# Turning the operands of an SSD stage in 32x32 blocks on VectorE and over DRAM, in place of TensorE transposes

## The chip, the core and the metric

The kernel runs on one core of a Trainium2 chip: TensorE (PE, with its weight loads shown as PEld), VectorE (DVE), ScalarE (ACT), GpSimd (POOL) and SyncE (SP), which here only starts transfers. The metric is the device time of one execution in microseconds (us).

## The reference

One layer of a generator: 256 latent and 256 context tokens of width 2048 (512 tokens in all) are normed and modulated, projected by `w_in`, passed through a two-way Mamba-2 scan (the SSD part: 32 heads in 8 groups, state 128, chunks of 128 tokens) and a gated MLP, and projected back. What matters here is the SSD part:

```python
z = h @ w_in                                   # 512 tokens, channels of x, B, C first
xbc = silu(dwconv(z[..., :XBC_W]))             # 5 taps along the tokens
# x: 2048 channels (256 a group), B and C: 128 channels a group
states = einsum('bckgn,bckgr,bckgrp->bcgrpn', B, decay_to_end, x * dt)   # sums over tokens k
h_starts = scan(states)                        # context first, then the latent chunks
y_diag = einsum('bcqgn,bckgn,bcgrqk,bckgrp->bcqgrp', C, B, L, x * dt)    # sums over tokens k
y_off  = einsum('bcqgn,bcgrpn,bcqgr->bcqgrp', C, h_starts, exp(acs))
y = y_diag + y_off + d_skip * x                # forward and backward in time, latent tokens only
```

The projection leaves channels on the partitions and tokens along the row. The sums over tokens want x and B with tokens on the partitions, so each is transposed; and the diagonal part comes out with channels on the partitions and is transposed back.

## The kernel before

**Projection.** Weights are kept as fp32 and split into a high and a low part (`hi_w` by ACT at L542, `lo_w` by DVE at L548, halves of 128x1024). A product of 128 channels by 512 tokens over 2048 inputs is 16 steps of three TensorE products each (`mm3`, L141 to L143): 48 products of 128x512, into one PSUM tile `psx`. The SSD stage lies between about 125 and 455 us. Its outer loop runs over 25 channel tiles (`REST`); seven more were projected earlier. Tile 4g and 4g+1 are x of group g, 4g+2 is B, 4g+3 is C; C tiles are of 256 latent tokens only, so their products are 128x256.

**Small work in between.** All that happens to a tile after its projection is put between the products of later tiles by a plan written by hand: `later(t, fn)` notes that `fn` is to be emitted `t` units from now, and `pump(dt)` after each six products moves the plan's clock by 1.3 units (0.65 for a C tile) and emits what is due. A tile of 48 products is so 10.4 units. The order in which instructions are emitted is kept on PE, DVE, ACT and POOL: each engine runs its list in that order and waits at the first instruction whose input is not there.

**One group.** `conv_tile` does the convolution: the middle tap on ACT (L607), the others on DVE (L623), silu on ACT (L626). Then:

- `ssd_x`: four TensorE transposes of 128x128 per x tile into PSUM (`ptx`, L742), which ACT copies to `xk` (L746); `xk` is x with tokens on the partitions.
- `ssd_w`: POOL scales `xk` to `xw` and `xl` (L754, L757); `ssd_sk`: POOL writes `d_skip * x` into `y` (L870).
- `ssd_b`: the same four transposes for B (`ptb`, L765; copy by ACT to `bk`, L770).
- `ssd_cb`: products of C and B (`pcb`, L808); `ssd_states`: products of `bk` with `xw` and `xl` (`psc` L825, `psl` L828). Then the states `hs`, the masks `M` and `E`, the products `pso` with C, and POOL's adds of those into `y` (`ssd_ya`).
- `ssd_yd`: the diagonal part (`psy`, L904); `ssd_yc`: ACT copies it to SBUF (`yc`); `ssd_yt`: four transposes (`pty`, L918); `ssd_yf`: DVE adds it to `y` (L922).

`plan_tile` (at the end of the listing) places these: B is transposed 7 units after its projection, the states come 6 units after C's (plus `late`, which is 10 for the first groups and 0 for the others).

The weights come by SP's queue (1 MB per tile). POOL's queue holds, in this stage, only `acs` (a table written to DRAM at L709) and `R` (its rows, read back to all partitions at L724, once per group). In a later stage of the same kernel the latent `y` and `vt` are turned in another way: DVE transposes 32x32 blocks within 128x512 (L1062, tile `T`), and 16 POOL transfers of 256 pieces of 128 B (L1067, tile `Z`) put the blocks to their places.

Of the kernel before, what the change touches and what calls it, by code (L numbers as in the profile page):

```python
# [8 lines left out]
F32 = mybir.dt.float32  # L9
# [11 lines left out]
NGRP = 8  # L21
# [26 lines left out]
def tile_hybrid_ssd_mlp(  # L48
# [47 lines left out]
    y = ypool.tile([P, 2, D], F32, tag="big16", name="y")  # L96
# [29 lines left out]
    dsk = cpool.tile([P, 32], F32, name="dsk")  # L126
# [45 lines left out]
    def spt(shape, name):  # L172
        return sps.tile(shape, F32, tag="s", name=name)
# [162 lines left out]
    for k in range(KT):  # L336
# [7 lines left out]
        g = k % 4  # L344
# [249 lines left out]
    def conv_tile(i, src, d0, ds):  # L594
        ch = ORDER[i]
        lat = ch >= 24
        n = 256 if lat else 512
        cw = pc[:, C_CW + 5 * i : C_CW + 5 * i + 5]
        l0 = 0 if lat else 256
        T = {}  # L600

        def tap0():
            if ch < 16:
                o = cv3.tile([P, n], F32, tag="xs", name=f"xbc{i}")
            else:
                o = cv2.tile([P, n], F32, tag="cs" if lat else "bs", name=f"xbc{i}")
            nc.scalar.activation(o, src, AF.Identity, bias=pc[:, C_CB + i : C_CB + i + 1], scale=cw[:, 2:3])  # L607
            T["o"] = o

        def taps():  # L610
            o = T["o"]
            o4 = o[:, l0 : l0 + 256].rearrange("p (r t) -> p r t", r=4)
            src4 = src[:, l0 : l0 + 256].rearrange("p (r t) -> p r t", r=4)
            for k in (0, 1, 3, 4):
                s = k - 2
                parts = [(o4, src4, 64)]
                if not lat:
                    parts.append((o[:, 0:256], src[:, 0:256], 256))
                for (a, z, w) in parts:
                    o0, o1 = max(0, -s), w - max(0, s)  # L620
                    ao = a[..., o0:o1]
                    zi = z[..., o0 + s : o1 + s]
                    nc.vector.scalar_tensor_tensor(ao, zi, cw[:, k : k + 1], ao, op0=ALU.mult, op1=ALU.add)  # L623

        def silu():
            nc.scalar.activation(T["o"], T["o"], AF.Silu)  # L626
            done[i] = T["o"]

        later(d0, tap0)
        later(d0 + 0.9, taps)  # L630
        later(d0 + ds, silu)
# [97 lines left out]
    gs_ = {}  # L729

    def hp(ap):
        return ap.rearrange("p (h q) -> p h q", h=4)

    def ssd_x(g, xi):
        S = gs_.setdefault(g, {})
        if xi == 0:
            S["xk"] = cv2.tile([P, 4, 256], F32, tag="xk", name=f"xk{g}")
        xk = S["xk"]
        xt = done.pop(4 * g + xi)
        p = spt([P, 4, P], f"ptx{g}{xi}")  # L740
        for t in range(4):
            nc.tensor.transpose(p[:, t, :], xt[:, t * P : (t + 1) * P], ident)  # L742
        S["ptx", xi] = p

    def ssd_xc(g, xi):
        nc.scalar.copy(gs_[g]["xk"][:, :, xi * P : (xi + 1) * P], gs_[g]["ptx", xi])  # L746

    def ssd_w(g):
        S = gs_[g]
        xk, h4 = S["xk"], slice(4 * g, 4 * g + 4)  # L750
        xw = cv1.tile([P, 2, 2, 256], F32, tag="xw", name=f"xw{g}")
        for t in range(2):
            for d in range(2):
                nc.gpsimd.tensor_tensor(hp(xw[:, t, d, :]), hp(xk[:, t, :]), bc(wctx(t, d)[:, h4], 2, 64), op=ALU.mult)  # L754
        xl = cv1.tile([P, 2, 256], F32, tag="xl", name=f"xl{g}")
        for d in range(2):
            nc.gpsimd.tensor_tensor(hp(xl[:, d, :]), hp(xk[:, 2 + d, :]), bc(wlt(d)[:, h4], 2, 64), op=ALU.mult)  # L757
        S["xw"], S["xl"] = xw, xl

    def ssd_b(g):  # L760
        bt = done[4 * g + 2]
        bk = cv1.tile([P, 4, P], F32, tag="bk", name=f"bk{g}")
        p = spt([P, 4, P], f"ptb{g}")
        for t in range(4):
            nc.tensor.transpose(p[:, t, :], bt[:, t * P : (t + 1) * P], ident)  # L765
        S = gs_.setdefault(g, {})
        S["bk"], S["ptb"] = bk, p

    def ssd_bc(g):
        nc.scalar.copy(gs_[g]["bk"], gs_[g]["ptb"])  # L770


    def ssd_d(g, c, h2):
# [91 lines left out]
    def yg(g, c):  # L865
        return y[:, c, g * 256 : (g + 1) * 256]

    def ssd_sk(g):
        for c in range(2):
            nc.gpsimd.tensor_tensor(hp(yg(g, c)), hp(gs_[g]["xk"][:, 2 + c, :]), bc(dsk[:, 4 * g : 4 * g + 4], 2, 64),  # L870
                                    op=ALU.mult)

    def ssd_o(g):
        S = gs_[g]
# [14 lines left out]
    def ssd_ya(g, c):  # L889
        yo = gs_[g]["yo", c]  # L890
        for d in range(2):
            nc.gpsimd.tensor_tensor(yg(g, c), yg(g, c), yo[:, d, :], op=ALU.add)
# [3 lines left out]
    def ssd_yd(g):  # L896
        S = gs_[g]
        E, xk = S["E"], S["xk"]
        ps = spt([P, 2, 2, P], f"psy{g}")
        for c in range(2):  # L900
            for q in range(2):
                for hh in range(2):
                    h = 2 * q + hh
                    nc.tensor.matmul(ps[64 * hh : 64 * hh + 64, c, q, :], lhsT=xk[:, 2 + c, h * 64 : (h + 1) * 64],  # L904
                                     rhs=E[:, c, h, :], start=True, stop=True)
        S["psy"] = ps

    def ssd_yc(g):
        S = gs_[g]
        S["yc"] = cv1.tile([P, 2, 2, P], F32, tag="M", name=f"yc{g}")  # L910
        nc.scalar.copy(S["yc"], S["psy"])

    def ssd_yt(g):
        S = gs_[g]
        S["pty"] = spt([P, 2, 2, P], f"pty{g}")
        for c in range(2):
            for q in range(2):
                nc.tensor.transpose(S["pty"][:, c, q, :], S["yc"][:, c, q, :], ident)  # L918

    def ssd_yf(g):  # L920
        ya = y[:, :, g * 256 : (g + 1) * 256]
        nc.vector.tensor_tensor(ya, ya, gs_[g]["pty"].rearrange("p c q k -> p c (q k)"), op=ALU.add)  # L922

    def plan_tile(i, src, d0=0.0, ds=5.2, tx=7.0, tw=1.5, late=0.0, td=0.0):

        g, r = divmod(i, 4)
        conv_tile(i, src, d0, ds)
        if r < 2:
            later(d0 + tx, lambda: ssd_x(g, r))
            later(d0 + tx + 0.7, lambda: ssd_xc(g, r))  # L930
        if r == 1:
            later(d0 + tx + tw, lambda: ssd_w(g))
            later(d0 + tx + tw + 3, lambda: ssd_sk(g))
        if r == 2:
            later(d0 + tx, lambda: ssd_b(g))
            later(d0 + tx + 0.7, lambda: ssd_bc(g))
        if r == 3:
            d0 += late
            for t, fn in [(6, ssd_cb), (6, ssd_states), (6.9, ssd_cbm), (7.6, lambda g: ssd_mb(g, 0)), (8, ssd_hc),
                          (8.7, ssd_hd), (9.4, ssd_hl), (9.5, lambda g: ssd_m(g, 0)), (11.2, lambda g: ssd_mb(g, 1)),  # L940
                          (12, ssd_o), (12.2, lambda g: ssd_m(g, 1)), (13.9, lambda g: ssd_yo(g, 0)),
                          (14.5, lambda g: ssd_yo(g, 1)), (14.7, lambda g: ssd_ya(g, 0)), (15.3, lambda g: ssd_ya(g, 1)),
                          (16 + td, ssd_yd), (16.9 + td, ssd_yc),
                          (18.6 + td, ssd_yt), (19.3 + td, ssd_yf)]:
                later(d0 + t, lambda fn=fn: fn(g))
            plan_d(d0 + 11, g + 1, 1.5)
            plan_e(d0 + 17, g + 1)
# [192 lines left out]
    for blk in range(16):  # L1140
# [85 lines left out]
    for i in range(8):  # L1226
        tk, b = divmod(i, 4)
# [156 lines left out]
```

## Time and profile before

| | before |
|---|---|
| median of 3 runs | 978.47 us (978.17 to 980.12) |
| profiled execution | 981.04 us, span 979.3 us, mean granted TensorE clock 0.996 |
| DVE, ACT, POOL busy | 68%, 51%, 19% of the span |
| a 1 MB weight load, issue to landing | 4.8 us (median of 25) |

In the rows of the trace the first number is the start in us, the second the time (of a group: all its instructions), then engine, line, operation, output<-inputs, shape and count; what stands in brackets is the idle time just ahead of it and what ended it. L12 is line 12 of the kernel that the row belongs to. The span runs from the first to the last instruction; the execution's time has some 1.7 us around it.

### The profile page before, as it was taken

The numbers are of one execution on the slowest core, as the hardware profiler recorded it, in microseconds if no ns is written. First come the engines' busy times: TensorE is split into PE (matmuls) and PEld (weight loads), VectorE is DVE, ScalarE is ACT, GpSimd is POOL, SyncE is SP. The second block draws the span as 40 slices with busy tenths as digits, with TensorE's granted clock in tenths as the row PEclk, the third lists the DMA queues.
The fourth block names the chain that finished last, engine by engine and source line by source line (L and its number), as shares of the span: only waits on it lengthen the run. The fifth ranks groups of instructions, "written<-read, shape, count | busy, mean of one in ns | idle before, by whom it ended". The sixth has DMA issues, their size and how long they took to land.

```text
span 979.3 us, 13757 instructions
## 1 busy us (share of the span) xinstructions
PE 968.3 (99%) x5242; PEld 781.8 (80%) x5242; DVE 665.1 (68%) x1075; ACT 496.0 (51%) x757; POOL 186.6 (19%) x290
## 2 busy tenths in 40 slices
PE   9999999999999999999999999999999999999997
PEld 4688888787887878787888888886888888888885
DVE  6888798778876665755766776666666665445636
ACT  4344458666565454645444443444566564345522
POOL 0000002541462122124000000043333451000000
PEclk9999999999999999999999999999999999999999
DMA  9999953332333423146787778785666666556722
GB/s 366 417 415 415 371 217 130 110 133 86 129 106 132 151 86 130 47 169 221 300 301 281 266 255 309 269 302 168 213 209 199 235 219 207 201 186 241 271 89 86
DMA packets 37090, 211.45 MB, mean 216 GB/s; under 512 B 6417, under 2 KB 6673, under 8 KB 14369
## 3 DMA queue, kind: packets, MB, share of 16 engines
q1 hardware_dynamic: 30240, 192.91, 53.2%
q0 software_dynamic: 6208, 16.85, 5.2%
q8 instruction: 41, 0.67, 0.3%
q10 hardware_dynamic: 576, 0.82, 0.2%
q14 instruction: 25, 0.20, 0.1%
HBM read 204.20 MB, written 2.16 MB: 211 GB/s over the span
## 4 chain that ended last, share of the span: by engine, by line
PE 78%; DMA 11%; DVE 6%; issue 3%; ACT 2%; POOL 0%; SPq 0%; DVEq 0%; ACTq 0%; POOLq 0%
PE psx L141 9%; PE psx L143 9%; PE psx L142 9%; PE pa L1159 7%; PE pa L1160 7%; PE pa L1161 7%; DMA gate<-in_wada_dram 5%; PE pm L1202 3%; PE pm L1201 3%; PE pm L1200 3%; DMA ada<-in_wada_dram 3%; DVE lo_w L88 3%; PE pq L1202 2%; PE pq L1201 2%; PE pq L1200 2%
## 5 line engine op out<-in xcount | busy, mean ns | idle before, releaser
L88 DVE TENSOR_TENSOR lo_w<-w,hi_w 128x1024 fp32r<-128x1024 f32 x173 | 209.7, 1221 | 127.9 <-ACT hi_w L87 127.9
L87 ACT CAST hi_w<-w 128x1024 fp32r<-128x1024 f32 x173 | 181.9, 1053 | 210.5 <-PE pa L1161 146.3
L1159 PE MATMUL pa<-hi_w,hhi 128*128 128x512 f32 x512 | 201.7, 394 | 0.0
L1160 PE MATMUL pa<-lo_w,hhi 128*128 128x512 f32 x512 | 200.2, 391 | 1.3 <-DVE lo_w L88 1.3
L1161 PE MATMUL pa<-hi_w,hlo 128*128 128x512 f32 x512 | 199.9, 390 | 0.0
L141 PE MATMUL psx<-hhi,hi_w 128*128 128x512 f32 (+1 forms) x400 | 153.4, 383 | 0.0
L143 PE MATMUL psx<-hhi,lo_w 128*128 128x512 f32 (+1 forms) x400 | 145.9, 365 | 0.0
L142 PE MATMUL psx<-hlo,hi_w 128*128 128x512 f32 (+1 forms) x400 | 145.7, 364 | 0.0
L1160 PEld LDWEIGHTS pa<-lo_w,hhi 128*128 128x128 f32 x512 | 96.4, 188 | 21.8 <-DVE lo_w L88 2.0
L1159 PEld LDWEIGHTS pa<-hi_w,hhi 128*128 128x128 f32 x512 | 96.5, 189 | 21.4 <-issue 1.6
L1161 PEld LDWEIGHTS pa<-hi_w,hlo 128*128 128x128 f32 x512 | 96.5, 189 | 20.3
L623 DVE SCALAR_TENSOR_TENSOR xbc<-psx,pc,xbc 128x248 f32<-128x248 f32 (+1 forms) x204 | 83.6, 471 | 34.5 <-ACT xbc L607 33.5
L548 DVE TENSOR_TENSOR lo_w<-w,hi_w 128x1024 fp32r<-128x1024 f32 x61 | 77.1, 1271 | 23.7 <-ACT hi_w L542 23.6
L1067 POOL DMA_DIRECT2D Z<-T x128 | 73.9, 584 | 97.4 <-DVE T L1062 28.8
L141 PEld LDWEIGHTS psx<-hhi,hi_w 128*128 128x128 f32 x400 | 75.5, 189 | 13.3 <-issue 2.9
L143 PEld LDWEIGHTS psx<-hhi,lo_w 128*128 128x128 f32 x400 | 75.4, 189 | 12.5
L142 PEld LDWEIGHTS psx<-hlo,hi_w 128*128 128x128 f32 x400 | 75.6, 189 | 12.2 <-issue 1.7
L542 ACT CAST hi_w<-w 128x1024 fp32r<-128x1024 f32 x61 | 63.5, 1044 | 26.0 <-PE psx L142 12.9
L1013 DVE SCALAR_TENSOR_TENSOR junk<-gate,cb 128x2048 bf16<-128x2048 f32 x16 | 36.7, 2291 | 27.9 <-DMA gate<-in_wada_dram 27.9
L1200 PE MATMUL pm<-hi_w,hhi 128*128 128x512 f32 x128 | 49.8, 389 | 0.0
L1201 PE MATMUL pm<-lo_w,hhi 128*128 128x512 f32 x128 | 49.8, 389 | 0.0
L1202 PE MATMUL pm<-hi_w,hlo 128*128 128x512 f32 x128 | 49.8, 389 | 0.0
(270 smaller groups left out, 1398.9 us busy)
## 6 DMA issues: line engine op xcount, KB each, us to landing
w<-in_wlat_dram SPq DMA_DIRECT2D x64, 1024.0 KB, 4.9
w<-in_wout_dram SPq DMA_DIRECT2D x32, 1024.0 KB, 4.8
w<-in_wxbc_dram SPq DMA_DIRECT2D x25, 1024.0 KB, 4.8
ada<-in_wada_dram SPq DMA_DIRECT2D x24, 1024.0 KB, 13.9
gate<-in_wada_dram SPq DMA_DIRECT2D x16, 1024.0 KB, 5.9
ada<-in_wada_dram SPq DMA_DIRECT2D x16, 512.0 KB, 12.3
R<-acs POOLq DMA_DIRECT2D x8, 1024.0 KB, 5.7
wst<-in_wst_dram SPq DMA_DIRECT2D x15, 480.0 KB, 12.9
```

Source lines behind the costliest of these rows:

```text
L87: nc.scalar.copy(hi, raw)
L88: nc.vector.tensor_tensor(lo, raw, hi.bitcast(F32), op=ALU.subtract)
L141: nc.tensor.matmul(ps, lhsT=whi, rhs=hhi[k][:, s], start=start, stop=False)
L142: nc.tensor.matmul(ps, lhsT=whi, rhs=hlo[k][:, s], start=False, stop=False)
L143: nc.tensor.matmul(ps, lhsT=wlo, rhs=hhi[k][:, s], start=False, stop=stop)
L623: nc.vector.scalar_tensor_tensor(ao, zi, cw[:, k : k + 1], ao, op0=ALU.mult, op1=ALU.add)
L1159: nc.tensor.matmul(pa[tk], lhsT=hhi[k][:, t], rhs=whi[:, w], start=k == 0, stop=False)
L1160: nc.tensor.matmul(pa[tk], lhsT=hhi[k][:, t], rhs=wlo[:, w], start=False, stop=False)
L1161: nc.tensor.matmul(pa[tk], lhsT=hlo[k][:, t], rhs=whi[:, w], start=False, stop=k == KT - 1)
L1200: nc.tensor.matmul(p, lhsT=yh[:, t], rhs=whi[:, w], start=j == 0, stop=False)
L1201: nc.tensor.matmul(p, lhsT=yh[:, t], rhs=wlo[:, w], start=False, stop=False)
L1202: nc.tensor.matmul(p, lhsT=yl[:, t], rhs=whi[:, w], start=False, stop=hf == 0 and j == 15)
```

## The change

x of groups 1 to 7, and B and y of groups 1 to 6, are no longer transposed by TensorE: 26 tiles of 128x512, 104 transposes, and the 26 copies by ACT. Instead `turn` has DVE transpose the tile in 32x32 blocks (`STREAM_TRANSPOSE`, into a tile `tt` of which there is one buffer; for y it reads PSUM and writes `yc`) and POOL write it to a scratch `D` in DRAM (two buffers), as 2048 pieces of 128 B. `turned` reads it back by four POOL transfers of 512 pieces of 128 B, one per 32 partitions, into `xk`, `bk` or a tile `yz`. Group 0, and B and y of group 7, stay on TensorE. `xk` gets another layout (x tile, token tile, channel) and its readers follow.

The plan moves with it: the reads are emitted 5 units (`LAND`) after the write, `xw` waits 13 units in place of 1.5 where x goes over DRAM, and `late` is at least 4 where B does, so that the states and all behind them come 4 units later in groups 2, 4, 5 and 6 (groups 1 and 3 had 10 and keep it).

```diff
+    def by_pe(g, what):
+        return g == 0 or g == NGRP - 1 and what != "x"
+
+    def turn(T, src, nm):
+        nc.vector.transpose(T.rearrange("p (b g c) -> p g b c", b=4, g=4), src.rearrange("p (g b c) -> p g b c", g=4, b=4))
+        D = drt.tile([64, 1024], F32, tag="D", name=f"D{nm}")
+        nc.gpsimd.dma_start(D.rearrange("(b g a) (i c) -> (a i) (b g) c", b=4, g=4, c=32),
+                            T.rearrange("p (u c) -> p u c", c=32))
+        return D
+
+    def turned(dst, D):
+        for b in range(4):
+            nc.gpsimd.dma_start(dst[32 * b : 32 * b + 32].rearrange("p (u c) -> p u c", c=32),
+                                D[16 * b : 16 * b + 16, :].rearrange("u (i c) -> i u c", c=32))
...
     def ssd_x(g, xi):
...
         xt = done.pop(4 * g + xi)
+        if not by_pe(g, "x"):
+            T = cv1.tile([P, 512], F32, tag="tt", name=f"tx{g}{xi}")
+            S["Dx", xi] = turn(T, xt, f"x{g}{xi}")
+            return
...
     def ssd_xc(g, xi):
-        nc.scalar.copy(gs_[g]["xk"][:, :, xi * P : (xi + 1) * P], gs_[g]["ptx", xi])
+        xk = gs_[g]["xk"][:, xi]
+        if by_pe(g, "x"):
+            nc.scalar.copy(xk, gs_[g]["ptx", xi])
+        else:
+            turned(xk.rearrange("p t c -> p (t c)"), gs_[g]["Dx", xi])
...
     def ssd_b(g):
+        if not by_pe(g, "b"):
+            T = cv1.tile([P, 512], F32, tag="tt", name=f"tb{g}")
+            S["Db"] = turn(T, bt, f"b{g}")
+            return
...
     def ssd_yc(g):
-        nc.scalar.copy(S["yc"], S["psy"])
+        if by_pe(g, "y"):
+            nc.scalar.copy(S["yc"], S["psy"])
+        else:
+            S["Dy"] = turn(S["yc"].rearrange("p c q k -> p (c q k)"), S["psy"].rearrange("p c q k -> p (c q k)"), f"y{g}")

     def ssd_yt(g):
+        if not by_pe(g, "y"):
+            S["pty"] = cv1.tile([P, 2, 2, P], F32, tag="yo0", name=f"yz{g}")
+            turned(S["pty"].rearrange("p c q k -> p (c q k)"), S["Dy"])
+            return
...
+    LAND = 5.0
+
     def plan_tile(i, src, d0=0.0, ds=5.2, tx=7.0, tw=1.5, late=0.0, td=0.0):
...
+        lx, lb, ly = (0.7 if by_pe(g, w) else LAND for w in "xby")
+        if lx == LAND:
+            tw = max(tw, 2 * LAND + 3)
+        if lb == LAND:
+            late = max(late, 4.0)
         if r < 2:
             later(d0 + tx, lambda: ssd_x(g, r))
-            later(d0 + tx + 0.7, lambda: ssd_xc(g, r))
+            later(d0 + tx + lx, lambda: ssd_xc(g, r))
...
         if r == 2:
             later(d0 + tx, lambda: ssd_b(g))
-            later(d0 + tx + 0.7, lambda: ssd_bc(g))
+            later(d0 + tx + lb, lambda: ssd_bc(g))
...
                           (16 + td, ssd_yd), (16.9 + td, ssd_yc),
-                          (18.6 + td, ssd_yt), (19.3 + td, ssd_yf)]:
+                          (16.9 + td + (1.7 if ly < 1 else LAND), ssd_yt), (18.6 + td + (0.7 if ly < 1 else 2 * LAND), ssd_yf)]:
```

How the lists read at the places that the prediction speaks of. Numbers behind a name tell buffers of one name apart; the first number is the group or, for `psx`, `xbc` and `lo_w`, the channel tile or the weight half.

TensorE before, in the tile after C of group 6 (`psx28`, whose products run over the inputs `hhi0` to `hhi15`):

```order
L143 MATMUL psx28_3764<-hhi9_125,lo_w43_3725 128x512
L808 MATMUL pcb6_3817<-xbc27_3771,xbc26_3699 128x128 x2
L825 MATMUL psc6_3820<-xw6_3678,bk6_3787 128x512 x2
L828 MATMUL psl6_3823<-xl6_3683,bk6_3787 128x256 x2
L141 MATMUL psx28_3764<-hhi10_126,hi_w43_3701 128x512
```

TensorE now:

```order
L143 MATMUL psx28_3800<-hhi15_131,lo_w43_3757 128x512
L848 MATMUL pcb6_3885<-xbc27_3807,xbc26_3732 128x128 x2
L865 MATMUL psc6_3888<-xw6_3840,bk6_3823 128x512 x2
L868 MATMUL psl6_3891<-xl6_3845,bk6_3823 128x256 x2
L141 MATMUL psx29_3894<-hhi0_116,hi_w44_3777 128x512
```

The states of group 6 stood after 30 of that tile's 48 products (`hhi9` is the tenth input), and stand after all 48.

DVE now, from the first split (`lo_w43`) in that tile on; `xbc27` are the taps of C, `tb6` the block transpose of B, `yz5` the diagonal part of group 5 back from DRAM:

```order
L968 TENSOR_TENSOR y_68<-y_68,yz5_3685 128x2x256
L549 TENSOR_TENSOR lo_w43_3757<-w21_3457,hi_w43_3734 128x1024
L549 TENSOR_TENSOR lo_w44_3791<-w22_3565,hi_w44_3777 128x1024
L624 SCALAR_TENSOR_TENSOR xbc27_3807<-psx27_3725,pc_87,xbc27_3807 128x4x62
L624 SCALAR_TENSOR_TENSOR xbc27_3807<-psx27_3725,pc_87,xbc27_3807 128x4x63 x2
L624 SCALAR_TENSOR_TENSOR xbc27_3807<-psx27_3725,pc_87,xbc27_3807 128x4x62
L549 TENSOR_TENSOR lo_w45_3821<-w22_3565,hi_w45_3809 128x1024
L739 STREAM_TRANSPOSE tb6_3824<-xbc26_3732 128x4x4x32
L549 TENSOR_TENSOR lo_w46_3865<-w23_3697,hi_w46_3857 128x1024
```

Before, the splits, the taps and the next split stood there in the same order, without the first row and without the transpose.

POOL before, from the last add of group 5 to the states of group 6 (`M60` is a mask, `hs6` the states):

```order
L892 TENSOR_TENSOR y_68<-y_68,yo51_3537 128x256 x2
L724 DMA R7_3586<-acs_1459 128x2048
L754 TENSOR_TENSOR xw6_3678<-xk6_3579,ed_1458 128x256 x4
L757 TENSOR_TENSOR xl6_3683<-xk6_3579,ed_1458 128x256 x2
L870 TENSOR_TENSOR y_68<-xk6_3579,dsk_108 128x256 x2
L853 TENSOR_TENSOR M60_3838<-cbb6_3835,dtt_1457 128x512
```

POOL now, the same stretch:

```order
L741 DMA Dy5_3643<-yc5_3641 128x16x32
L725 DMA R7_3650<-acs_1461 128x2048
L747 DMA xk6_3590<-Dx60_3593 32x16x32 x4
L747 DMA yz5_3685<-Dy5_3643 32x16x32 x4
L741 DMA Dx61_3711<-tx61_3709 128x16x32
L747 DMA xk6_3590<-Dx61_3711 32x16x32 x4
L741 DMA Db6_3826<-tb6_3824 128x16x32
L786 TENSOR_TENSOR xw6_3840<-xk6_3590,ed_1460 128x256 x4
L789 TENSOR_TENSOR xl6_3845<-xk6_3590,ed_1460 128x256 x2
L747 DMA bk6_3823<-Db6_3826 32x16x32 x4
```

`xw6` and `xl6` now stand behind eleven transfers of POOL, the write of B last among them, and the four reads of `bk6` follow them. In group 2 the write of the next x stands between:

```order
L741 DMA Db2_2420<-tb2_2418 128x16x32
L786 TENSOR_TENSOR xw2_2436<-xk2_2143,ed_1460 128x256 x4
L789 TENSOR_TENSOR xl2_2441<-xk2_2143,ed_1460 128x256 x2
L741 DMA Dx30_2458<-tx30_2456 128x16x32
L747 DMA bk2_2417<-Db2_2420 32x16x32 x4
```

Before, no transfer stood there but those of `R`.

More of the change, by code (lines that the diff above doesn't have):

```diff
@@ L516, in tile_hybrid_ssd_mlp @@
     drp = ctx.enter_context(mkpool(name="drp", bufs=1, space=bass.MemoryType.DRAM))
+    drt = ctx.enter_context(mkpool(name="drt", bufs=2, space=bass.MemoryType.DRAM))
     cv1 = cvs.enter_context(mkpool(name="cv1", bufs=1))
@@ L736, in ssd_x @@
         if xi == 0:
-            S["xk"] = cv2.tile([P, 4, 256], F32, tag="xk", name=f"xk{g}")
-        xk = S["xk"]
+            S["xk"] = cv2.tile([P, 2, 4, P], F32, tag="xk", name=f"xk{g}")
         xt = done.pop(4 * g + xi)
+        if not by_pe(g, "x"):
+            T = cv1.tile([P, 512], F32, tag="tt", name=f"tx{g}{xi}")
+            S["Dx", xi] = turn(T, xt, f"x{g}{xi}")
+            return
         p = spt([P, 4, P], f"ptx{g}{xi}")
@@ L745, in ssd_xc, with xtok_, hx, hb @@
     def ssd_xc(g, xi):
-        nc.scalar.copy(gs_[g]["xk"][:, :, xi * P : (xi + 1) * P], gs_[g]["ptx", xi])
+        xk = gs_[g]["xk"][:, xi]
[3 more added lines that the diff above has]
+            turned(xk.rearrange("p t c -> p (t c)"), gs_[g]["Dx", xi])
+    def xtok_(g, t):
+        return gs_[g]["xk"][:, :, t].rearrange("p x (h q) -> p x h q", h=2)
+    def hx(ap):
+        return ap.rearrange("p (x h q) -> p x h q", x=2, h=2)
+    def hb(ap):
+        return bc(ap.rearrange("p (x h) -> p x h", x=2), 3, 64)
     def ssd_w(g):
         S = gs_[g]
-        xk, h4 = S["xk"], slice(4 * g, 4 * g + 4)
+        h4 = slice(4 * g, 4 * g + 4)
         xw = cv1.tile([P, 2, 2, 256], F32, tag="xw", name=f"xw{g}")
@@ L753, in ssd_w @@
             for d in range(2):
-                nc.gpsimd.tensor_tensor(hp(xw[:, t, d, :]), hp(xk[:, t, :]), bc(wctx(t, d)[:, h4], 2, 64), op=ALU.mult)
+                nc.gpsimd.tensor_tensor(hx(xw[:, t, d, :]), xtok_(g, t), hb(wctx(t, d)[:, h4]), op=ALU.mult)
         xl = cv1.tile([P, 2, 256], F32, tag="xl", name=f"xl{g}")
         for d in range(2):
-            nc.gpsimd.tensor_tensor(hp(xl[:, d, :]), hp(xk[:, 2 + d, :]), bc(wlt(d)[:, h4], 2, 64), op=ALU.mult)
+            nc.gpsimd.tensor_tensor(hx(xl[:, d, :]), xtok_(g, 2 + d), hb(wlt(d)[:, h4]), op=ALU.mult)
         S["xw"], S["xl"] = xw, xl
@@ L761, in ssd_b @@
         bt = done[4 * g + 2]
-        bk = cv1.tile([P, 4, P], F32, tag="bk", name=f"bk{g}")
+        S = gs_.setdefault(g, {})
+        S["bk"] = cv1.tile([P, 4, P], F32, tag="bk", name=f"bk{g}")
+        if not by_pe(g, "b"):
+            T = cv1.tile([P, 512], F32, tag="tt", name=f"tb{g}")
+            S["Db"] = turn(T, bt, f"b{g}")
+            return
         p = spt([P, 4, P], f"ptb{g}")
@@ L765, in ssd_b @@
             nc.tensor.transpose(p[:, t, :], bt[:, t * P : (t + 1) * P], ident)
-        S = gs_.setdefault(g, {})
-        S["bk"], S["ptb"] = bk, p
+        S["ptb"] = p
     def ssd_bc(g):
-        nc.scalar.copy(gs_[g]["bk"], gs_[g]["ptb"])
+        bk = gs_[g]["bk"]
+        if by_pe(g, "b"):
+            nc.scalar.copy(bk, gs_[g]["ptb"])
+        else:
+            turned(bk.rearrange("p t c -> p (t c)"), gs_[g]["Db"])
     def ssd_d(g, c, h2):
@@ L869, in ssd_sk @@
         for c in range(2):
-            nc.gpsimd.tensor_tensor(hp(yg(g, c)), hp(gs_[g]["xk"][:, 2 + c, :]), bc(dsk[:, 4 * g : 4 * g + 4], 2, 64),
-                                    op=ALU.mult)
+            nc.gpsimd.tensor_tensor(hx(yg(g, c)), xtok_(g, 2 + c), hb(dsk[:, 4 * g : 4 * g + 4]), op=ALU.mult)
     def ssd_o(g):
@@ L903, in ssd_yd @@
                     h = 2 * q + hh
-                    nc.tensor.matmul(ps[64 * hh : 64 * hh + 64, c, q, :], lhsT=xk[:, 2 + c, h * 64 : (h + 1) * 64],
+                    nc.tensor.matmul(ps[64 * hh : 64 * hh + 64, c, q, :], lhsT=xk[:, q, 2 + c, hh * 64 : (hh + 1) * 64],
                                      rhs=E[:, c, h, :], start=True, stop=True)
@@ L910, in ssd_yc @@
         S["yc"] = cv1.tile([P, 2, 2, P], F32, tag="M", name=f"yc{g}")
-        nc.scalar.copy(S["yc"], S["psy"])
+        if by_pe(g, "y"):
+            nc.scalar.copy(S["yc"], S["psy"])
+        else:
+            S["Dy"] = turn(S["yc"].rearrange("p c q k -> p (c q k)"), S["psy"].rearrange("p c q k -> p (c q k)"), f"y{g}")
     def ssd_yt(g):
         S = gs_[g]
+        if not by_pe(g, "y"):
+            S["pty"] = cv1.tile([P, 2, 2, P], F32, tag="yo0", name=f"yz{g}")
+            turned(S["pty"].rearrange("p c q k -> p (c q k)"), S["Dy"])
+            return
         S["pty"] = spt([P, 2, 2, P], f"pty{g}")
```

## The prediction

> **What bounds the kernel now.** I read the page first, then the SSD stage (about 125 to 455 us) by stretches, since the edits lie only there.
>
> ```profile
> PE 968.3 (99%) x5242; PEld 781.8 (80%) x5242; DVE 665.1 (68%) x1075; ACT 496.0 (51%) x757; POOL 186.6 (19%) x290
> PEclk9999999999999999999999999999999999999999
> 200.00:240.00 40.00, 40.00 (x214) 32.60 (x213) 30.53 (x62) 24.93 (x45) 12.09 (x17) 1.00 0.28 106
> 400.00:440.00 40.00, 40.00 (x217) 33.28 (x216) 24.23 (x41) 20.84 (x29) 8.89 (x13) 1.00 0.37 132
> ```
>
> The columns of the last two are the stretch, its length, busy time of PE, PEld, DVE, ACT and POOL, the granted clock, the DMA share and GB/s. TensorE is never idle in these 40 us and runs at full clock. DVE has 9 to 16 us of room, POOL 28, ACT 15. So whatever is taken from TensorE's list shortens the kernel one for one, and any moment at which TensorE must wait lengthens it one for one. A transfer costs nothing until TensorE's next instruction needs it.
>
> **What the removed work is worth.** The timeline of PE around one removed turn, and the one wait that goes with it:
>
> ```profile
> 260.33 0.39 PE L142 MATMUL psx<-hlo,hi_w 128*128 128x512 f32 x1
> 260.56 0.40 PE L143 MATMUL psx<-hhi,lo_w 128*128 128x512 f32 x1
> 260.79 0.60 PE L742 MATMUL ptx<-ident,xbc 128*128 128x128 f32 x4
> 261.15 0.47 PE L141 MATMUL psx<-hhi,hi_w 128*128 128x512 f32 x1
> 261.46 0.39 PE L142 MATMUL psx<-hlo,hi_w 128*128 128x512 f32 x1
> PE ptx L742 <- ACT xbc L626: 0.5, 1, 0.5
> ```
>
> Matmuls are pipelined, so I count starts, not durations. Products of 128x512 start 0.23 us apart (260.33 to 260.56). From 260.56 to 261.46 are 0.90 us, in which two products (0.45) and the four transposes stand: 0.45 us for a turn. Of x there are 2 x 7 turns, of B 6, of y 6: 26 x 0.45 = 11.7 us. The wait at `ptx` (x of group 1, 0.5 us) goes too. Gain: 12.2 us. The 26 copies by ACT that go are worth nothing: ACT is not waited for elsewhere on this path.
>
> **What is added, and what hides it.** DVE gets 26 block transposes, POOL 26 writes and 104 reads of DRAM. On average there is room. For x of groups 2 to 7, used a tile or more later, and for y, which only `yf` on DVE awaits, I take 0: POOL's and DVE's idle time covers it. Not so for B: `bk` is an operand of the states `psc`, and TensorE takes its list in order. In the new order `psc` of groups 2, 4, 5 and 6 stands behind all 48 products of the tile after C (before: behind 30). Group 6, on the clock of the old trace:
>
> ```profile
> 380.22 0.40 PE L141 MATMUL psx<-hhi,hi_w 128*128 128x512 f32 x1
> 387.53 0.60 PE L808 MATMUL pcb<-xbc,xbc 128*128 128x128 f32 x4
> 387.97 1.02 PE L825 MATMUL psc<-xw,bk 128*128 128x512 f32 x2
> ```
>
> That tile begins at 380.22. 48 x 0.227 (10.9) bring `pcb` to 391.1, and its 0.44 (387.53 to 387.97) bring `psc` to 391.55. That is when `bk6` is due. What stands ahead of it:
>
> ```profile
> 378.60 2.35 DVE L548 TENSOR_TENSOR lo_w<-w,hi_w 128x1024 fp32r<-128x1024 f32 x2
> 381.03 2.02 DVE L623 SCALAR_TENSOR_TENSOR xbc<-psx,pc,xbc 128x248 f32<-128x248 f32 x4
> 382.96 1.22 DVE L548 TENSOR_TENSOR lo_w<-w,hi_w 128x1024 fp32r<-128x1024 f32 x1
> L922 DVE TENSOR_TENSOR y<-y,pty x8: 674/687/690, 192.3 to 454.2; 128x512 f32<-128x512 f32 x8
> L1062 DVE STREAM_TRANSPOSE T<-vt x8: 666/702/712, 642.3 to 713.9; 128x512 f32<-128x512 f32 x8
> 372.59 2.33 POOL L754 TENSOR_TENSOR xw<-xk,ed 128x256 f32<-128x256 f32 x4 [10.31 <-ACT xk L746]
> 374.89 1.18 POOL L757 TENSOR_TENSOR xl<-xk,ed 128x256 f32<-128x256 f32 x2
> L1067 POOL DMA_DIRECT2D Z<-T x128: 584/584/612, 647.1 to 812.0; - x128
> L709 POOL DMA_DIRECT2D acs<-y x1: 651/651/651, 135.3 to 135.3; - x1
> ```
>
> In DVE's new order `yf` of group 5 (0.69) stands ahead of the two splits, so these run from 379.3 to 381.6, the C taps (2.02) to 383.6, `lo_w45` (1.22) to 384.8, and `tb6`, priced as the transposes of the later stage (0.70), to 385.5. POOL issues `Db6` (0.58) till 386.1, and then must do `xw6` and `xl6` (2.33 + 1.18) before its four reads of `bk6`: 389.6. The reads need `Db6` landed.
>
> Issue times: the Z transfers have 256 pieces of 128 B each, `acs` 32 pieces, and the issue takes 0.58 against 0.65 us. No row has 512 or 2048 pieces; I take 0.58 flat as the nearest, and keep growth with the pieces as a rival. Landing, from issue:
>
> ```profile
> out_dram<-xf SPq DMA_DIRECT2D x5, 256.0 KB, 2.4
> acs<-y POOLq DMA_DIRECT2D x1, 64.0 KB, 5.1
> Z<-T POOLq DMA_DIRECT2D x16, 32.0 KB, 7.1
> DMA to landing us min/median/max: 1.8/4.2/8.4
> ```
>
> For `Db6` (256 KB in 128 B pieces) the nearest bounds are 2.4 (same bytes, coarse pieces, quiet) and 7.1 (the same small pieces while four weight loads were in flight, 642 to 660 us; the last row is Z over the whole kernel). I take 5.1, the write to DRAM from POOL in this very stage, which like `Db6` shares the engines with one weight load: 390.6. Four issues from there: the last begins 1.73 later, at 392.3. It reads 64 KB with no weight load then in flight: 1.8 to 4.2, I take 2.5: 394.8. So TensorE waits 394.8 - 391.55 = 3.2 us (1.6 to 7.0).
>
> - Group 5 has the same order: 3.2.
> - Group 4: the four reads of `yz3` (2.3) stand on POOL ahead of `xw4`, so its reads start at 391.9; the last is issued at 393.6 and landed at 396.1: 4.6 (3.9 to 7.0).
> - Group 2: no `yf` ahead, so `tb2` ends at 384.8. But the write `Dx30` stands on POOL ahead of the reads of `bk2`, and needs `tx30`, which DVE can only write once `Db2` has landed, since both use one buffer (`tt`): 389.9, 390.6, 391.2, last issue 392.9, landed 395.4: 3.9 (1.5 to 7.6). Behind `tx30` on DVE waits the split `lo_w20` (1.22): 391.8, while its first product stands a whole tile of 10.9 us behind `psc2`: 0.
> - Groups 1 and 3 have `late=10` where the others have 4: 6 units, at 1.3 units per six products 6/1.3 x 6 x 0.227 = 6.3 us later than the 391.55, which covers 3.2 to 4.6: 0. Group 7 keeps TensorE for B and y: 0.
>
> Sum of waits 3.2 + 3.2 + 4.6 + 3.9 = 14.9 us (8.6 to 28.6). Behind a waiting `psc` stand `psl` and the next tile's 48 products, so all that follows shifts by the full wait; the other engines use it to catch up, but TensorE has no slack later that would give it back.
>
> **What a wait does to the clock.** The trace has it once, after two waits close together:
>
> ```profile
> 671.98 0.50 PE L1160 MATMUL pa<-lo_w,hhi 128*128 128x512 f32 x1 [0.51 <-DVE lo_w L88]
> 674.27 0.49 PE L1046 MATMUL pg<-gd,g 48*128 48x512 f32 x1 [0.85 <-DVE gd L1042]
> 674.00:675.00 1.00, 0.73 (x2) 0.48 (x3) 1.00 (x2) 0.00 (x0) 1.00 (x3) 0.99 1.14 156
> 675.00:676.00 1.00, 1.00 (x4) 0.73 (x3) 1.00 (x2) 0.00 (x0) 1.00 (x3) 0.50 0.87 352
> 676.00:677.00 1.00, 1.00 (x4) 0.81 (x3) 1.00 (x2) 0.00 (x0) 1.00 (x3) 0.50 0.97 377
> 677.00:678.00 1.00, 1.00 (x3) 0.77 (x3) 0.69 (x2) 0.56 (x1) 0.73 (x2) 0.50 0.94 320
> 678.00:679.00 1.00, 1.00 (x5) 0.70 (x3) 0.48 (x1) 0.49 (x1) 0.00 (x0) 0.81 1.12 336
> ```
>
> Idle 0.51 and 0.85 us, and from 675 on the granted clock is 0.50 till 678.4. Each stretch loses one minus its clock: 0.01 + 0.50 + 0.50 + 0.50 + 0.19 = 1.7 us. The waits forecast here are two to four times as long, so I take one such drop behind each: 4 x 1.7 = 6.8 us (0 to 6.8).
>
> The Trainium skill, page "TensorE: Matmul & The Clock Gate", Part 1, states that a whole idle window of about 3.4 us halves the rate and a busy one restores it. By it only the waits of groups 2 and 4 would count, 3.4 us, and the sum below would be 6.1 instead of 9.5. The row speaks against its first half (1.36 us of idleness were enough) and agrees with the second (3.4 us at 0.50); I stay with the row.
>
> **The sum.** -12.2 + 14.9 + 6.8 = +9.5 us, against the profiled execution's 981.04 (span 979.3): 990.5. The median of the runs shown, 978.47, is 2.6 lower, and I take the difference over to it: 988.0. By the bounds -12.2 + 8.6 + 0 = -3.6 to -12.2 + 28.6 + 6.8 = +23.2: 974.9 to 1001.7.
>
> **Rivals.** A change under 0.2% (2 us) can't be told from none.
>
> Faster: short landings. If `Db` lands within 3.4 us and a read in 1.8, POOL's arithmetic alone sets the reads, the waits are 1.6 + 1.6 + 3.9 + 1.5 = 8.6, and if they pass without a clock drop the time is 974.9. For it: the out rows' 2.4, and the 1.8 of Z. Against it: 2048 small pieces, and waits longer than those that dropped the clock. It decides where waits and drops together come under 12.2 us; two drops already cancel the gain. A variant comes out by a page's price: the Trainium skill, "DMA: Bandwidth & Descriptors", section "Anatomy of one DMA", fits 2.0 us + bytes/436e3 per transfer from POOL. My estimate from that fit is 2.6 us for the write and 2.15 for a read, waits of 9.8 and, without drops, 976.1; no row of this trace has such a transfer alone, and I give it a third of this rival's chance.
>
> Slower by far: POOL becomes the bound. If the issue grows with the pieces (0.584 per 256), a write takes 4.7 and a read 1.2 us, a turn 4.7 + 4 x 1.17 = 9.4, and the four turns of a group 37.5. With the 9 to 12 us of arithmetic that POOL does in 40 us now that is 47 to 50 us, more than the 40, and `bk` comes later from group to group: for the groups 4 to 6, which follow each other, 3 x 7 to 3 x 10, and 4 to 15 for group 2, so +25 to +45 in place of +9.5: 1003 to 1023. For it: nothing in the rows, since 32 and 256 pieces cost alike. Against it: just that; but 256 to 2048 is a long way.
>
> The change doesn't do what it says: TensorE's list is shorter by exactly the 104 transposes, so no.
>
> **How the numbers follow.** Likeliest, waits for `bk` with some drops (980 to 1002): 0.60, and 988.0 is its sum. POOL bound: 0.16. Short landings: 0.24, of which 0.16 are faster than 976.5 (the bounds and the page's fit, 0.08 each) and 0.08 within 0.2% (one drop of the clock on top, 976.6). Slower holds 0.60 + 0.16 = 0.76. The range leaves out the low end of the short landings and the upper half of the POOL case: 974 to 1014; the likeliest case alone has 980 to 1002.
>
> **What would show it.** In the new trace: TensorE's products at the same 0.23 us spacing with no `ptx`, `ptb`, `pty` in groups 1 to 6; idle time of TensorE ahead of `psc` four times, of 3 to 5 us, released by the transfers of `bk`, and none in groups 1, 3 and 7; the granted clock under 1 behind each; the writes' issue near 0.58 us; `STREAM_TRANSPOSE` near 0.70, also where it reads PSUM. I am wrong if `Db` lands in under 3 us, if waits of 3 us leave the clock at 1.00, if the issue of 2048 pieces takes several us, or if DVE, held up at the single `tt` buffer by a late landing, delays a weight split, which would add waits at products of 128x512 anywhere in the stage.

## The result and the profile after

The changed kernel takes 1018.04 us (median of 6, 1016.38 to 1028.69) against 979.19 (6 runs): ratio 1.0418, interval 1.0374 to 1.0462. Slower, as forecast, but by 39 us where 9.5 were forecast, and outside the range. The profiled execution took 1016.38 us, span 1014.7, against 981.04 and 979.3: 35.4 us more in the span. (The profiled execution of before is among the slower ones of its kernel, that of after the fastest of six, so the medians lie further apart.)

The page's busy row after, and the two stretches shown of before:

```profile
PE 966.2 (95%) x5138; PEld 776.0 (76%) x5138; DVE 681.9 (67%) x1101; ACT 481.7 (47%) x731; POOL 288.2 (28%) x420
200.00:240.00 40.00, 32.16 (x172) 26.13 (x170) 28.92 (x55) 21.41 (x36) 24.17 (x32) 1.00 0.50 152
400.00:440.00 40.00, 35.40 (x170) 28.90 (x169) 25.44 (x49) 15.57 (x21) 23.49 (x32) 0.96 0.59 177
```

The 104 transposes are gone (5242 matmuls to 5138), and TensorE now stands idle for 4.6 to 7.8 us of each stretch. The waits of PE in the SSD stage (us in total, times, longest), and the five at `psc`:

```profile
PE psc L865 <- DMA bk<-Db: 28.7, 4, 9.6
PE psc L865 <- POOL xw L786: 6.4, 1, 6.4
PE pso L917 <- DVE hs L887: 2.1, 1, 2.1
PE psx L141 <- DVE xbc L624: 1.8, 2, 1.2
PE psx L141 <- ACT xbc L608: 0.7, 1, 0.7
...
245.12 1.19 PE L865 MATMUL psc<-xw,bk 128*128 128x512 f32 x1 [9.63 <-DMA bk<-Db]
286.38 1.22 PE L865 MATMUL psc<-xw,bk 128*128 128x512 f32 x1 [6.35 <-POOL xw L786]
328.62 1.19 PE L865 MATMUL psc<-xw,bk 128*128 128x512 f32 x1 [9.12 <-DMA bk<-Db]
380.74 1.19 PE L865 MATMUL psc<-xw,bk 128*128 128x512 f32 x1 [5.40 <-DMA bk<-Db]
431.61 1.19 PE L865 MATMUL psc<-xw,bk 128*128 128x512 f32 x1 [4.60 <-DMA bk<-Db]
```

These are groups 2, 3, 4, 5 and 6, 35.1 us. With the four shorter waits (4.6) that is 39.7 us where 14.9 were forecast. Each of the five is followed by half clock; here group 6 (columns as in the stretches above):

```profile
431.00:432.00 1.00, 0.39 (x1) 0.42 (x2) 1.00 (x1) 0.00 (x0) 1.00 (x2) 0.80 0.00 0
432.00:433.00 1.00, 1.00 (x2) 0.42 (x2) 0.12 (x1) 0.00 (x0) 1.00 (x1) 0.50 0.00 0
433.00:434.00 1.00, 1.00 (x2) 0.34 (x1) 0.00 (x0) 0.00 (x0) 0.02 (x1) 0.50 0.86 164
434.00:435.00 1.00, 1.00 (x2) 0.34 (x1) 0.00 (x0) 0.00 (x0) 0.00 (x0) 0.50 0.92 385
435.00:436.00 1.00, 1.00 (x6) 0.81 (x5) 0.00 (x0) 0.71 (x2) 0.05 (x1) 0.99 0.95 401
```

One minus the clock, times PE's busy time in each stretch of 1 us, is 1.6 us here (0.20 x 0.39 + 3 x 0.50 + 0.01), and 10.5 over the five.

The account: 39.7 of waits + 10.5 of half clock - 12.2 of transposes = 38.0. The next stage's products begin at 466.4 in place of 426.5, 39.9 later (weight loads of `pa`: first and last start):

```profile
L1159 PEld LDWEIGHTS pa<-hi_w,hhi x512: 186/188/329, 426.5 to 795.8; 128*128 128x128 f32 x171
L1212 PEld LDWEIGHTS pa<-hi_w,hhi x512: 186/188/192, 466.4 to 831.2; 128*128 128x128 f32 x171
```

1.9 us are not accounted for. That stage is then 4.5 us shorter than before (364.8 against 369.3), since the waits and the half clock that the prediction quoted from 668 to 679 us (1.3 + 0.9 + 1.7) happen not to occur in it; so the span grows by 35.4.

### The profile page after: what moved, and what is told of

It is laid out like the page before. It is cut to its first block, busy times and chain, and to the rows that moved or that the text cites. A ratio compares the mean times of both kernels' runs of the same rounds, so it can differ in the third digit from the quotient of the medians.

```text
span 1014.7 us, 13752 instructions
## 1 busy us (share of the span) xinstructions
PE 966.2 (95%) x5138; PEld 776.0 (76%) x5138; DVE 681.9 (67%) x1101; ACT 481.7 (47%) x731; POOL 288.2 (28%) x420
## 3 DMA queue, kind: packets, MB, share of 16 engines
q0 software_dynamic: 11616, 30.49, 10.5%
## 4 chain that ended last, share of the span: by engine, by line
PE 76%; DMA 9%; POOL 6%; DVE 4%; issue 3%; ACT 1%; SPq 0%; POOLq 0%; DVEq 0%; ACTq 0%
PE pa L1212 12%; PE pa L1213 11%; PE pa L1214 11%; PE psx L141 5%; PE psx L142 5%; PE psx L143 5%; DMA ada<-in_wada_dram 4%; PE pm L1254 3%; PE pm L1253 3%; PE pm L1255 3%; PE pq L1254 2%; PE pq L1253 2%; PE pq L1255 2%; DMA Dx<-tx 2%; PE psc L865 2%
## 5 line engine op out<-in xcount | busy, mean ns | idle before, releaser
L143 PEld LDWEIGHTS psx<-hhi,lo_w 128*128 128x128 f32 x400 | 75.5, 189 | 12.3
L865 PE MATMUL psc<-xw,bk 128*128 128x512 f32 x32 | 24.1, 895 | 35.1 <-DMA bk<-Db 28.7
## 6 DMA issues: line engine op xcount, KB each, us to landing
ada<-in_wada_dram SPq DMA_DIRECT2D x16, 512.0 KB, 12.3
```

The source lines that it names most:

```text
L143: nc.tensor.matmul(ps, lhsT=wlo, rhs=hhi[k][:, s], start=False, stop=stop)
```

## The experiments

Theory A: a turn over DRAM costs nothing by itself; TensorE loses because its in-order list comes to `psc` before `bk` or `xw` is there, and the clock drops behind each long wait. Its rival, theory B: POOL and DVE can't carry 26 turns, so whatever is moved is late again.

**States later.**

```diff
-            late = max(late, 4.0)
+            late = max(late, 10.0)
```

> All groups with B over DRAM get late=10 in place of 4 for groups 2, 4, 5 and 6: 6 units, about 6.3 us of products, later states. Theory A (the loss is TensorE standing at psc because its place in the order comes too early for bk, and the clock drops behind it): the waits of groups 2, 4, 5, 6 (9.6, 9.1, 5.4, 4.6) shrink by 6.3 each to about 3.3, 2.8, 0, 0, the 6.4 of group 3 (which waits for xw and is not moved) stays or shrinks, two or three clock drops are left: 1018 - 22.6 - 3 = about 992, range 980 to 998. Theory B (POOL or DVE cannot carry the 26 turns, so lateness grows from group to group and whatever is moved waits again): above 1005.

Measured 998.57 us (991.32 to 1004.75), ratio 1.0194 (1.0133 to 1.0254), just above the range expected. The page is that of the slowest execution, 1004.75 us. At `psc` 35.1 us became 12.2, but `pso` behind the states and the taps waited 10.8:

```profile
PE psc L865 <- DMA bk<-Db: 9.2, 3, 3.8
PE pso L917 <- DVE hs L887: 7.0, 3, 3.3
PE psx L141 <- DVE xbc L624: 3.8, 4, 1.2
PE psc L865 <- POOL xw L786: 3.0, 2, 2.1
```

The next stage began at 443.3 in place of 466.5, so more than half of the loss in the SSD stage was a matter of the place, as theory A says; what came new is lateness of the lists, as theory B says. Another 7 us of this execution lie behind the stage, which took 559.8 us from there on against 552.7 before.

**B back on TensorE, B alone, y back on TensorE.** The condition of `by_pe`, in this order (the first also keeps `late` at 4):

```diff
-        return g == 0 or g == NGRP - 1 and what != "x"
+        return g == 0 or what == "b" or g == NGRP - 1 and what != "x"
+        return g == 0 or g == NGRP - 1 or what != "b"
+        return g == 0 or what == "y" or g == NGRP - 1 and what != "x"
```

> B back on TensorE (6 of 26 turns), x and y still over DRAM, the states kept 4 units later as in the changed kernel. Theory A: no wait for bk, so 28.7 us of waits and four clock drops (6.8) go, and 6 x 0.45 = 2.7 us of transposes come back: 1018 - 28.7 - 6.8 + 2.7 = 985; if the wait of group 3 for xw goes too (POOL is freed of Db and bk), 977. Theory B (POOL's list is the bound): still above 1000, with waits for xw at psc in several groups.

> Only B over DRAM (6 turns), x and y on TensorE, so POOL and DVE have nearly their old lists. Theory A (the way from the B tile to bk is by itself longer than the plan leaves): waits at psc of about 3 us in groups 4, 5, 6 and 3 to 6 in group 2, each with a clock drop of 1.7, against a gain of 2.7: 979 - 2.7 + 13.5 + 6.8 = about 997, range 988 to 1002. Theory B (the other 20 turns make it late): waits under 1 us, about 977.

> y back on TensorE (6 turns), x and B over DRAM. Theory A with POOL's order as the cause of what the forecast missed: group 3 waits no more for xw (the write and reads of y and their landing, 1.2 + 2.4 + 2.6 us, stood ahead of it), group 4 2.6 less, one clock drop less, 2.7 of transposes back: 1018 - 6.4 - 2.6 - 1.7 + 2.7 = about 1010. If y is what loads POOL beyond measure, 995 or lower; if it plays no part, 1020.

Measured: without B 989.05 us (ratio 1.0117, 1.0065 to 1.0169); B alone 1009.02 (1.0301, 1.0286 to 1.0317); without y 1010.85 (1.0323, 1.0295 to 1.0352). The waits at `psc` of the three:

```profile
PE psc L865 <- POOL xw L786: 9.0, 4, 7.6
```

```profile
PE psc L865 <- DMA bk<-Db: 23.8, 4, 10.7
```

```profile
PE psc L865 <- DMA bk<-Db: 26.3, 4, 10.8
PE psc L865 <- POOL xw L786: 2.9, 1, 2.9
```

Without B theory A had expected 985, and theory B over 1000. The wait of 7.6 there is group 3's for `xw`: the transfers of B are not its cause. Six turns of B alone bring three quarters of the loss (30 of 39 us), more than the 988 to 1002 us that were expected of them, so theory A had the direction and not the size. With POOL and DVE almost as free as in the kernel before, the way of B is seen by itself, in group 6 (block transpose on DVE, then POOL's transfers; TensorE comes to `pcb` at 416.77):

```profile
409.73 0.70 DVE L739 STREAM_TRANSPOSE tb<-xbc 128x512 f32<-128x512 f32 x1
410.74 1.23 POOL L741 DMA_DIRECT2D Db<-tb  x1 [7.89 <-DVE tb L739]
416.61 2.58 POOL L747 DMA_DIRECT2D bk<-Db  x4 [4.64 <-DMA Db<-tb]
416.77 0.60 PE L848 MATMUL pcb<-xbc,xbc 128*128 128x128 f32 x4
```

`psc` starts at 420.99, 10.6 us after `tb` is written (410.4): 0.3 to the issue, 5.9 till the reads, 1.9 for three issues, and 2.5 from the last issue on (the last read landed after 2.3). Group 6 leaves it 6.8. In group 4 it takes 15.7 (301.5 to 317.2): the write landed after 6.9 us, and the last read after 5.4, beside a weight load (311.6 to 316.8). Without y, group 3's wait for `xw` halves: y's transfers are part of POOL's list there, not all of it. That the time came out at the 1010 expected is partly luck, since group 3 was to wait no more, and group 4's wait grew from 9.1 to 10.8 where it was to shrink by 2.6.

**x alone, y alone.** Here the states keep their old place, and for x `xw` comes 8.5 units behind in place of 13.

```diff
+        return g == 0 or what != "x"
-            tw = max(tw, 2 * LAND + 3)
+            tw = max(tw, 8.5)
```

```diff
+        return g == 0 or g == NGRP - 1 or what != "y"
```

> Only x over DRAM (14 turns), B and y on TensorE, states at their old place (late as before), xw 8.5 units behind the second x tile's turn so that it comes before the states. Theory A (a turn costs nothing where TensorE's next use is far): gain 14 x 0.45 + 0.5 = 6.8, no clock drop, 972; a wait for xw in group 3 as in the run with B on TensorE (7.6) would make it 980. Theory B (turns cost TensorE's time wherever they are, by DVE's and POOL's lists): above 982.

> Only y over DRAM (6 turns). No instruction of TensorE reads yz, so theory A: gain 6 x 0.45 = 2.7, 976.2, no wait at psc. Theory B (DVE stands at its add of yz and is late for the next weight split or taps): 980 or more.

Measured: x alone 980.26 us (ratio 1.0018, 0.9992 to 1.0043), y alone 975.49 (0.9964, 0.9951 to 0.9977). y is free, as theory A has it: the only wait of PE in the stage is the old 0.5. x is not, and the 972 expected failed: nine waits of up to 1.4 us (`xw` 2.7, taps 1.8, `hs` 1.4, `E` 1.3), 7.2 together, eat the gain of 6.8, without a clock drop in the stage. In the profiled execution (987.79 us, well above the median) the stage ended 2.8 us later than before; the waits explain 0.4 of it, and the rest stays open. The 980 expected for a long wait of group 3 for `xw` was met without one (0.4 us there).

**The transfers on SP's queue; the same with later states; and B's own buffer.**

```diff
-        nc.gpsimd.dma_start(D.rearrange(
+        nc.sync.dma_start(D.rearrange(
-            nc.gpsimd.dma_start(dst[32 * b : 32 * b + 32]
+            nc.sync.dma_start(dst[32 * b : 32 * b + 32]
...
-            late = max(late, 4.0)
+            late = max(late, 10.0)
...
-            T = cv1.tile([P, 512], F32, tag="tt", name=f"tb{g}")
+            T = cv1.tile([P, 512], F32, tag="tb", name=f"tb{g}")
```

> All 26 turns as in the changed kernel, but the writes to DRAM and the reads are issued from SP's queue, not POOL's. Theory A1 (about half of the missed waits is POOL's list: issues of 1.17 and 0.65 us, arithmetic and waits for R and for earlier transfers ahead of the reads): waits of 4 to 7 in groups 2 and 4, 2 to 3 in 5 and 6, none in 3, with four clock drops: about 992. Theory A2 (the waits are the landing times alone): 1010 to 1018. If SP's weight loads stand in front of the reads or are delayed by them, above 1018.

> As the run on SP's queue, with the states of groups 2, 4, 5 and 6 another 6 units later. Theory A: no wait for bk or xw is left, the removed transposes show: 979 - 12.2 + 1 to 3 = about 969. Theory B (turns over DRAM cost more than they save wherever they are put): above 979.

> As the run on SP's queue with late=10, and B's block transpose has a buffer of its own, so the first x of the next group no longer waits on DVE for the landing of B's write. Theory A: what is left of waits there (0.7 in group 2, 1.6 in group 4, 0.8 at the taps) falls by 1 to 3: 967 to 970. If the single buffer costs nothing any more: 970.

Measured: 993.38 us (ratio 1.0145, 1.0129 to 1.0161), 970.16 (0.9921, 0.9896 to 0.9946) and 968.58 (0.9894, 0.9879 to 0.9908). The waits of PE in the stage, of the first and of the last:

```profile
PE psc L865 <- DMA bk<-Db: 19.7, 4, 9.1
PE psc L865 <- POOL xw L786: 1.4, 2, 1.0
```

```profile
PE psc L865 <- DMA bk<-Db: 0.9, 1, 0.9
PE psx L141 <- DVE xbc L624: 0.8, 1, 0.8
PE psy L943 <- DVE E L903: 0.7, 1, 0.7
PE pso L917 <- DVE hs L887: 0.4, 1, 0.4
```

Off POOL's list the wait of group 3 for `xw` falls to 1.4, and groups 5 and 6 wait 1.9 and 1.3. Groups 2 and 4 still wait 7.3 and 9.1, more than the 4 to 7 expected, and the clock fell twice, not four times, so the sum came near 992 by errors that cancel. With the later place as well, 4.5 us of waits stay, and with B's own buffer 2.8, without half clock: 2.8 - 12.2 = -9.4, and the stage ended 8.4 us earlier than before. The intervals of the last two overlap, so what the buffer brings by itself isn't clear. The last version is 1% faster than the kernel before: with the transfers off POOL's list DVE carries all 26 turns, and theory B doesn't hold there.

**Control: the kernel before with the later states.**

```diff
+            if 0 < g < NGRP - 1:
+                late = max(late, 10.0)
             d0 += late
```

> Control: the kernel before, nothing turned over DRAM, only the states of groups 1 to 6 put at late=10, as in the best run so far. If the later place costs nothing and brings nothing, 979 within 0.2%, and the gain of 9 us of the run on SP's queue is the removed transposes alone. If the later place brings something by itself (an engine's list evened out), 973 to 976; if it costs, above 982.

Measured 978.69 us (ratio 0.9993, 0.9983 to 1.0003): the place itself is free, so the gain above is not the place's but that of the transposes.

**R's loads on SP's queue.** In the changed kernel POOL's list ahead of `xw3` (285.13) reads so, and then come `yz2` and the first write of group 4:

```profile
264.12 1.18 POOL L741 DMA_DIRECT2D Dx<-tx  x1 [0.32 <-DVE tx L739]
270.77 0.56 POOL L725 DMA_DIRECT2D R<-acs  x1 [5.47 <-issue]
272.67 1.17 POOL L741 DMA_DIRECT2D Dy<-yc  x1 [1.34 <-DVE yc L739]
273.83 2.58 POOL L747 DMA_DIRECT2D bk<-Db  x4
276.40 1.93 POOL L747 DMA_DIRECT2D xk<-Dx  x3
280.75 0.65 POOL L747 DMA_DIRECT2D xk<-Dx  x1 [2.42 <-DMA Dy<-yc]
```

```diff
-        nc.gpsimd.dma_start(R.rearrange(
+        nc.sync.dma_start(R.rearrange(
```

> The changed kernel, with R's loads (1 MB per group) issued from SP's queue, nothing else. In the changed kernel POOL stands 5.5 us at the issue of R of group 4 and 2.4 us at a read behind the landing of y's write, both ahead of xw of group 3, for which TensorE waits 6.4. Theory A (POOL's in-order list is the cause of that wait): it falls to 0 to 1 with its clock drop, the others stay: 1018 - 6 - 2.6 = about 1009. If the list is not the cause: 1016 to 1020.

Measured 1023.23 us (ratio 1.0446, 1.0408 to 1.0485), and group 3 still waits 5.8. Its SSD stage ended at 465.7, 0.8 us earlier than in the changed kernel; that this execution (1025.07 us) is longer comes from the stages behind it, whose length differs among the 13 traces (548.1 to 559.8 us). The expectation failed: R was not what POOL stood for. Without it the next row stands, for the same reason, that DVE has not come so far:

```profile
271.88 1.15 POOL L741 DMA_DIRECT2D Dy<-yc  x1 [7.31 <-DVE yc L739]
```

## Why the prediction was wrong

The mechanism was right in its main parts: the gain of 12.2 (the last run on SP's queue shows it to about 1 us, and the control that it is not the place), TensorE standing at `psc` for `bk` in groups 2, 4, 5 and 6, half clock behind each of these waits, and y without a wait of TensorE. The term that failed is "the sum of waits", 14.9 against 39.7, outside even its bound of 28.6. Of the 24.8 that it lacked, groups 2 and 4 have 10.2, group 3 6.4, groups 5 and 6 3.6, and waits elsewhere 4.6. By its own steps:

- **Groups 5 and 6** (forecast 3.2 each; 5.4 and 4.6). The deadline was right: `pcb` starts 5.9 and 5.7 us after `tb` is written (forecast 391.1 - 385.5 = 5.6). The way to `bk` took 11.9 and 10.9 us against 9.3. In group 6:

```profile
420.01 0.70 DVE L739 STREAM_TRANSPOSE tb<-xbc 128x512 f32<-128x512 f32 x1
421.00 1.16 POOL L741 DMA_DIRECT2D Db<-tb  x1 [3.09 <-DVE tb L739]
422.18 3.26 POOL L786 TENSOR_TENSOR xw<-xk,ed 128x256 f32<-128x256 f32 x4
425.41 1.17 POOL L789 TENSOR_TENSOR xl<-xk,ed 128x256 f32<-128x256 f32 x2
427.23 2.60 POOL L747 DMA_DIRECT2D bk<-Db  x4 [0.66 <-DMA Db<-tb]
```

  The landing of the write set the start of the reads: it took 5.7 in place of 5.1 (in group 5 6.8), and the first read began 0.5 later. The issue of the write took 1.16 us in place of 0.58 "flat", a read's 0.65, and `xw` 3.26 in place of 2.33, but POOL was through with `xw` and `xl` 0.66 before the reads began. The last read landed after 2.3 (forecast 2.5).
- **Groups 2 and 4** (forecast 3.9 and 4.6; 9.6 and 9.1). This is where most went wrong. `pcb` starts only 2.0 and 2.2 us after `tb` is written, where 6.3 and 5.6 were put, and the way to `bk` took 12.3 and 12.0 us, where 10.6 was put. DVE's place was taken from group 6 for all four. In group 2 the taps of an x tile stand ahead of `tb` on DVE, and the trace of before shows what that leaves:

```profile
228.27 1.22 DVE L548 TENSOR_TENSOR lo_w<-w,hi_w 128x1024 fp32r<-128x1024 f32 x1
229.86 0.60 PE L808 MATMUL pcb<-xbc,xbc 128*128 128x128 f32 x4
```

  A transpose of 0.70 behind this split ends at 230.2, and `pcb`, 18 products (4.1) later in the new order, starts at 234.0: 3.8, as the run with B alone has it (3.8). The other step that failed is DVE's own lateness, which was put at nothing; it makes 2.0 of the 3.8 in group 2. In group 4 the distance was 4.4 with B alone, 3.2 with x as well and 2.2 with x and y. There DVE stood 2.6 us for a mask `M` that stands on POOL behind the write of an x tile, and its list has no gap from there on, with `yc` in it and the tail of group 3 (which has `late=10` and so falls there):

```profile
299.89 1.20 POOL L741 DMA_DIRECT2D Dx<-tx  x1 [3.15 <-DVE tx L739]
301.10 1.05 POOL L893 TENSOR_TENSOR M<-cbb,dtt 128x512 f32<-128x512 f32 x1
302.19 1.14 DVE L901 SCALAR_TENSOR_TENSOR M<-cbf,dtt,M 128x128 f32<-128x128 f32 x4 [2.60 <-POOL M L893]
...
304.57 3.18 DVE L624 SCALAR_TENSOR_TENSOR xbc<-psx,pc,xbc 128x248 f32<-128x248 f32 x8
...
309.40 0.70 DVE L739 STREAM_TRANSPOSE yc<-psy 128x512 f32<-128x512 f32 x1
...
315.95 0.71 DVE L739 STREAM_TRANSPOSE tb<-xbc 128x512 f32<-128x512 f32 x1
```

  `Dx30` behind the single buffer was as forecast: `tx30` waited 5.2 us for `Db2`, and the reads of `bk2` began 8.0 us after `tb2`'s end (forecast 6.4).
- **Group 3** (forecast 0; 6.4). Its deadline for `bk` was rightly far, 20.5 us after `tb3`; even so `bk3` landed at 281.5, 1.5 us after TensorE came, since POOL issued its reads 10.9 us after `Db3` had landed. The longer wait was for `xw3`, an operand from x, which the prediction had put at 0. It stands on POOL behind seventeen transfers counted from `Db3` on; the forecast had counted what stands ahead of `bk` alone.
- **The other waits** (forecast 0; 4.6): `pso` and the taps, from DVE's and POOL's lateness.
- **The clock** (forecast 4 x 1.7 = 6.8; 10.5): five drops in place of four, and 2.1 each, since some lasted longer. But the row on which it rested misled: the runs here have 45 waits of TensorE between 0.5 and 2.8 us in this stage, none with a drop; of four between 2.9 and 3.6 three had one; all 20 above 3.6 had one. That each wait had its drop is so in part owed to waits longer than forecast. The Trainium skill's rule of an idle window of about 3.4 us ("TensorE: Matmul & The Clock Gate", Part 1) agrees with these. What dropped the clock after 1.36 us of waits at 675 us stays open: in later stages of the runs it fell four more times behind two short waits of 1.7 to 2.2 us together, but the first run on SP's queue has nearly the same pair (0.51 and 0.87, at 686 and 688 us) at full clock.
- **POOL as the bound** did not come: 32 to 2048 pieces take 0.58 to 1.2 us to issue, not 4.7. The measured time lies within this rival's 1003 to 1023, but not by its cause. **Short landings** did not come either; the Trainium skill's fit ("DMA: Bandwidth & Descriptors", "Anatomy of one DMA") gave an estimate of 2.6 us for the write, where this median is 5.3, and 2.15 for a read, where it is 2.3:

```profile
Db<-tb POOLq DMA_DIRECT2D x6, 256.0 KB, 5.3
bk<-Db POOLq DMA_DIRECT2D x24, 64.0 KB, 2.3
```

## What to carry to other kernels

A transfer is free only if every consumer's place in an in-order list is later than its whole way, and that way is to be summed for each instance by itself: three of the five waits were missed because one group's list, taken to be on time, stood for all. Ask of each operand of the waiting instruction, not of the moved one alone. Where the bound engine has no slack, move the deadline (here free) and keep the transfers off a queue whose engine computes; neither alone was enough here (998.6 and 993.4 us), both together brought the 1%.

## What was not expected of the hardware

- The way of 256 KB through DRAM, from the end of the block transpose to the landing of the last read, took 10.4 us from POOL's queue where POOL did nothing else meanwhile (B alone, group 6), and 3.2 of it were issues. From SP's queue the issue of B's write took 0.38 us and its landing 3.2 to 3.5, that of a read 3.1 to 3.5 (medians). Whether larger pieces would land sooner was not tried.
- Landings are longer beside loads in flight. In the eight runs whose turns go by POOL, the 223 reads with no load of weights or of `R` beside them (less than 0.5 us of overlap) landed after 2.1 to 3.3 us, median 2.3; the 353 others after up to 9.5, median 4.7.
- POOL's ninth transfer in a row started only when the one eight before it had landed (280.75, behind `Dy`). In no trace does a POOL transfer start before the one eight before it has landed. Whether the program or the queue sets this was not tried.
